# Norm vectors, dump tiles and memory tiles move into shared buffers, and the raw weight ring grows from three buffers to five

## The chip, the cores and the metric

The kernel runs on one core of a Trainium2 chip. The engines that matter here are TensorE (PE for its matmuls, PEld for its weight loads), VectorE (DVE), ScalarE (ACT), GpSimd (POOL), and SyncE (SP), whose queue issues nearly all DMA transfers. The metric is the device time in microseconds; for each kernel the median of several runs is compared. One further execution is profiled, and the profile and trace are of that one.

## The reference

A decoder trunk of four layers works on one sequence of 256 positions, 1024 wide, in float32. Each layer is a half-step SwiGLU feed-forward network (FFN), a token mixer that also attends to a memory of 256 rows, and a second half-step FFN, each between two RMS norms ("sandwich"). The mixer's kind changes with the layer (a gated spatial mix, dilated window attention, attention with forget gates, and the first again).

```python
def rms_norm(x, g):
    xf = x.astype(jnp.float32)
    y = xf * lax.rsqrt(jnp.mean(xf * xf, axis=-1, keepdims=True) + RMS_EPS)
    return (y * g.astype(jnp.float32)).astype(x.dtype)

def swiglu_ffn(x, w_gate_up, w_down):
    gate, up = jnp.split(x @ w_gate_up, 2, axis=-1)
    return (jax.nn.silu(gate) * up) @ w_down

def reference(...):
    for i in range(DEPTH):
        g = norm_g[i]
        x = x + 0.5 * rms_norm(swiglu_ffn(rms_norm(x, g[0]), ffn_w_gate_up[i, 0], ffn_w_down[i, 0]), g[1])
        h = rms_norm(x, g[2])
        mem_n = rms_norm(mem, mem_norm_g[i])
...
        x = x + rms_norm(y, g[3])
        x = x + 0.5 * rms_norm(swiglu_ffn(rms_norm(x, g[4]), ffn_w_gate_up[i, 1], ffn_w_down[i, 1]), g[5])
    return x
```

The FFN is 2816 wide. Every weight is read once; weights are most of the 360 MB that the kernel reads.

## The kernel before

**Weight units.** Weights arrive in units of 128 partitions by up to 1024 float32 (512 KB). A matmul in float32 precision is made of three faster ones: each weight is split into `hi` (ACT, line 309) and `lo` = weight - `hi` (DVE, line 310), and each activation likewise, and `hi*hi`, `hi*lo` and `lo*hi` are summed (`mm3`, lines 332 to 336; the FFN's down product at 684; the seven-product sets at 615). So each unit costs one DMA, one ACT and one DVE instruction, and 12 matmuls of 512 columns in most places.

**Two rings.** A unit is first loaded into a `raw` buffer (`RAW` = 3, `load_next`, line 242, issued by SP at line 240), then split into one of ten pairs `hi`, `lo` (`RING` = 10, `split_next`, line 288). Splitting a unit frees its raw buffer and issues the next load. `slot` (line 320) is called after each unit's matmuls: it releases ring places, issues one load of a quad if any is due, runs one job of the background list `bg`, and lets `pump` split up to two units, at most nine ahead of what PE has released.

**An FFN** (`ffn`, line 529) runs over six column sets of the gate and up weights, s = 0 to 5. Sets 0, 1, 3 take four gate and four up units each. Sets 2 and 4 (`SEVEN`) use a scheme of seven products instead of eight (`seven`, line 626): eight weight tiles ("quads", four tiles of two halves, loaded whole) are added and subtracted in place by DVE (line 277), and seven combinations are multiplied with prepared sums of activations (`sums`, line 593: S1 to S4, each split into a pair of tiles `sh`, `sl`). The quads live in the tiles tagged `rows`, `mgh`, `mgl` (of the main pool) and `q22` (of the FFN's own pool). In `seven` snapshots of partial sums go to four tiles tagged `snap`; `c11` (line 635), `c22`, `c21` and `c12` (lines 653 to 659) combine them on DVE. Set 5 has four mixed units (`half("e", ...)`, its product at line 719). Down products (22 units "D") are filled in between: 4 in set 1, 2 in set 3, 4 in each of the seven sets, and the last 8 at the end, which are held in the ring and passed over twice, first for the rows t = 0 and then for t = 1. Between the two passes `boundary` runs the norm for t = 0 and during the first units of what follows for t = 1.

**The norm** (`ln_stages`, line 356) has four steps: ACT squares the product into a `junk` dump, of which only the row sum is used (373), while DVE multiplies it by the vector `gpost` into `rows` (374); DVE adds it to x (378); ACT squares x into a dump (381); DVE scales by `gpre` into `rows` (385). POOL computes the reciprocal roots (348, 349). Then PE transposes `rows` (399). After mixers and after second FFNs the transposed result is also kept in four tiles `xf` of tag `snap`, for `sums`.

**Norm vectors.** `gain` (line 351) allots a tile `gpost` or `gpre` (one buffer each, in the main pool, 4 KB a partition) and issues a 512 KB load that repeats a vector over the partitions. In an FFN the job `gains` (line 667) is put on `bg` right after `sums`, in the first FFN after set 2; in a mixer both are loaded after the memory keys and values.

**Memory.** In the first FFN, after set 2, `setup2` (line 453) loads constants and the memory's rows (into the `gpost` buffer) and computes their norms. In each first FFN, after set 4, `mem_gained` (line 752) loads the transposed memory in eight pieces of 128 KB (`memraw`, two buffers) and splits them into `mgh`, `mgl`.

**What sets the order.** The program's order is a priority. The tile library lays out each engine's queue ahead of time from a model of durations and of buffers becoming free, so an instruction can stand earlier in its queue than in the text, but each queue runs in its order on the chip: an instruction that waits holds up all behind it. That includes SP's queue of loads.

Of the kernel before, what the change touches and what calls it, by code (L numbers as in the profile page):

```python
# [10 lines left out]
F32 = mybir.dt.float32  # L11
F32R = mybir.dt.float32r
I32 = mybir.dt.int32
BF16 = mybir.dt.bfloat16
AF = mybir.ActivationFunctionType
# [3 lines left out]
P = 128  # L19
SEQ = 256  # L20
D = 1024
# [11 lines left out]
RING = 10  # L33
RAW = 3
HELD = 8
# [168 lines left out]
class Trunk:  # L204
# [145 lines left out]

    def gain(self, l, n, tag):
        t = self.main.tile([P, D], F32, tag=tag, name=tag)
        self.nc.sync.dma_start(out=t, in_=self.io["norm_g"][l, n].partition_broadcast(P))
        return t

    def ln_stages(self, st, t, ps, post_scale, post_eps, gpost, gpre):
        nc = self.nc
        if "rows" not in st:
            st["rows"] = None
        junk = lambda: self.main.tile([P, D], BF16, tag="junk", name="junk")  # L360
        ss = self.small.tile([P, 1], F32, tag="ss", name="ss", bufs=8)
        r = self.small.tile([P, 1], F32, tag="r", name="r", bufs=8)
        ss2 = self.small.tile([P, 1], F32, tag="ss2", name="ss2", bufs=8)
        r2 = self.small.tile([P, 1], F32, tag="r2", name="r2")
        x = self.x[t]

        def rows():
            if st["rows"] is None:
                st["rows"] = self.main.tile([P, 2, D], F32, tag="rows", name="rows")
            return st["rows"][:, t, :]  # L370

        def s1():
            nc.scalar.activation(out=junk(), in_=ps, func=AF.Square, scale=post_scale, accum_out=ss)  # L373
            nc.vector.tensor_tensor(out=rows(), in0=ps, in1=gpost, op=ALU.mult)  # L374
            self.rsqrt(r, ss, post_eps)

        def s2():
            nc.vector.scalar_tensor_tensor(out=x, in0=rows(), scalar=r, in1=x, op0=ALU.mult, op1=ALU.add)  # L378

        def s3():  # L380
            nc.scalar.activation(out=junk(), in_=x, func=AF.Square, scale=1 / 32, accum_out=ss2)
            self.rsqrt(r2, ss2, self.eps1)

        def s4():
            nc.vector.scalar_tensor_tensor(out=rows(), in0=x, scalar=r2, in1=gpre, op0=ALU.mult, op1=ALU.mult)

        out = []
        if ps is not None:
            out += [s1, s2]
        if gpre is not None:  # L390
            out += [s3, s4]
        return out
# [36 lines left out]
    def setup(self):  # L429
# [3 lines left out]
        nc.sync.dma_start(out=self.x[0], in_=io["x"][:P, :])  # L433
        self.gpre = self.gain(0, 0, "gpre")
        nc.sync.dma_start(out=self.ident, in_=io["ident"])
# [17 lines left out]
    def setup2(self):  # L453
        nc, io, c = self.nc, self.io, self.const
        self.tri1 = c.tile([P, SEQ], F32, name="tri1")
        self.R = c.tile([P, SEQ], F32, name="R")

        def loads():
            nc.sync.dma_start(out=self.tri1, in_=io["tri1"])
            nc.sync.dma_start(out=self.mg, in_=io["mem_g"])  # L460

        def squares(t):
            m = self.main.tile([P, D], F32, tag="gpost", name="memrow")
            nc.sync.dma_start(out=m, in_=io["mem"][t * P:(t + 1) * P, :])
            ss = self.small.tile([P, 1], F32, tag="ss", name="ss", bufs=8)
            nc.scalar.activation(out=self.main.tile([P, D], BF16, tag="junk", name="junk"), in_=m, func=AF.Square,
                                 scale=1 / 32, accum_out=ss)
            self.rsqrt(self.r_mem[:, t:t + 1], ss, self.eps1)

        def inverse():  # L470
            ps = self.rot()
            for t in range(2):
                d = self.main.tile([P, SEQ], F32, tag="memraw", name="memf", bufs=2)
                nc.vector.tensor_scalar(out=d[:, :P], in0=self.ident, scalar1=self.r_mem[:, t:t + 1], scalar2=None,
# [54 lines left out]
    def ffn(self, l, f, post_next, pre_next, last=False):  # L529
        nc, tc = self.nc, self.tc  # L530
        with tc.tile_pool(name=f"ffn{l}{f}", bufs=1, reuse_waits="tile") as fp:
# [61 lines left out]
            def sums():  # L593
# [3 lines left out]
                for dst, a, b, op in ((x22, x21, x22, ALU.subtract), (x21, x11, x21, ALU.subtract),  # L597
                                      (x11, x22, x11, ALU.subtract), (x12, x12, x11, ALU.add)):
                    tt(out=dst, in0=a, in1=b, op=op)
                    y = tuple(fp.tile([P, 4, P], F32R, tag=n, name=n, bufs=4) for n in ("sh", "sl"))  # L600
                    self.split(*(v.rearrange("p a b -> p (a b)") for v in y), dst)
# [65 lines left out]
            def gains():  # L667
                gn["post"] = self.gain(l, post_next[0], "gpost")
                if pre_next:
                    gn["pre"] = self.gain(*pre_next, "gpre")  # L670

            if (l, f) != (0, 0):
                self.bg.append(gains)
            ys = [self.acc() for _ in range(2)]
# [26 lines left out]
            for s in range(1, SETS):  # L701
# [3 lines left out]
                if s in SEVEN:  # L705
                    seven(s)
                    if s == min(SEVEN) and (l, f) == (0, 0):
                        self.bg.extend(self.setup2() + [gains])
                    if s == min(SEVEN) and (l, f) == (0, 1):
# [37 lines left out]
    def mem_chunk(self, k):  # L747
        m = self.main.tile([P, SEQ], F32, tag="memraw", name="memraw", bufs=2)
        self.nc.sync.dma_start(out=m, in_=self.io["mem_t"][k * P:(k + 1) * P, :])
        return m  # L750
# [211 lines left out]
    def gains(self, l):  # L962
        return self.gain(l, 3, "gpost"), self.gain(l, 4, "gpre")

# [364 lines left out]
```

## Time and profile before

| | |
|---|---|
| median of 3 runs | 1900.68 us |
| lowest, highest run | 1900.43, 1908.29 us |
| the profiled execution's own time | 1902.04 us |
| span of its instructions | 1900.2 us |
| PE, DVE, ACT busy | 98%, 80%, 57% of the span |
| granted TensorE clock | 0.999 |
| DMA | 362.65 MB, mean 191 GB/s |
| raw loads, quad loads | 515, 128 |

The page gives busy shares, groups of instructions by line and a chain of work; other views of the same trace list waits, windows and the timeline. In a list of waits each row reads "engine, what it was about to write, line <- what ended the wait: total us, times, longest us". In a table of windows the columns are the window, the busy time of PE, PEld, DVE, ACT and POOL (with counts), the granted clock, the DMA engines' busy share and GB/s. A matmul's duration is modelled: consecutive matmuls overlap in the records.

### The profile page before, as it was taken

What the parts mean: (1) busy time and instruction counts of PE and PEld (TensorE: products, weight loads), DVE (VectorE), ACT (ScalarE), POOL (GpSimd) and SP (SyncE); (2) the same over time, 40 slices, a digit from 0 to 9 for tenths busy, and PEclk for the clock granted to TensorE, in tenths of its full rate; (3) what the DMA queues carried; (4) which work ended last, traced back from release to release, by engine and by line L of the source; (5) the groups of instructions that cost most, each with busy time, mean ns of one, the idle gap of its engine ahead of it and who ended that gap; (6) DMA issues with size and microseconds to landing.
All of it is one profiled execution on the core that took longest, in us unless ns stands there. A gap on an engine that the chain in (4) does not pass through costs nothing.

```text
span 1900.2 us, 25015 instructions
## 1 busy us (share of the span) xinstructions
PE 1858.8 (98%) x9406; PEld 1550.4 (82%) x9406; DVE 1514.9 (80%) x1828; ACT 1085.9 (57%) x1469; POOL 59.8 (3%) x115
## 2 busy tenths in 40 slices
PE   7999999999999999999999999999999999999998
PEld 5888888787878897888888889888888878988886
DVE  6987888896879768889697966878877886878894
ACT  5655656564656545655565656555556555656562
POOL 0000100000000000000000000000000000100000
PEclk9999999999999999999999999999999999999999
DMA  8646747545663663754566357275476535747632
GB/s 295 235 167 200 233 156 266 205 140 176 233 222 115 199 203 111 266 198 145 180 231 233 112 185 238 102 246 184 151 229 227 189 127 183 243 156 244 220 105 86
DMA packets 103865, 362.65 MB, mean 191 GB/s; under 512 B 12084, under 2 KB 16576, under 8 KB 103616
## 3 DMA queue, kind: packets, MB, share of 16 engines
q1 hardware_dynamic: 103568, 359.47, 56.5%
q8 instruction: 74, 1.21, 0.3%
q0 software_dynamic: 176, 1.59, 0.2%
q14 instruction: 47, 0.39, 0.1%
HBM read 359.95 MB, written 1.06 MB: 190 GB/s over the span
## 4 chain that ended last, share of the span: by engine, by line
PE 60%; DVE 17%; DMA 12%; ACT 5%; issue 4%; POOL 1%; ACTq 0%; SPq 0%; DVEq 0%
PE acc L684 15%; DMA raw<-in_w 12%; PE rot L615 9%; PE rot L334 9%; PE rot L336 9%; PE rot L335 9%; DVE lo L310 9%; ACT hi L309 4%; DVE quad L277 3%; PE acc L944 3%; PE rot L557 1%; PE rot L399 1%; PE rot L848 1%; DVE x L378 1%; PE rot L880 1%
## 5 line engine op out<-in xcount | busy, mean ns | idle before, releaser
L310 DVE TENSOR_TENSOR lo<-raw,hi 128x1024 fp32r<-128x1024 f32 (+1 forms) x515 | 624.4, 1219 | 216.9 <-ACT hi L309 207.5
L309 ACT ACTIVATE hi<-raw 128x1024 fp32r<-128x1024 f32 (+1 forms) x515 | 542.1, 1055 | 397.0 <-DMA raw<-in_w 259.0
L334 PE MATMUL rot<-hi,xth 128*128 128x512 f32 (+3 forms) x1072 | 414.9, 387 | 2.5 <-ACT hi L309 1.6
L336 PE MATMUL rot<-hi,xtl 128*128 128x512 f32 (+3 forms) x1072 | 411.6, 384 | 1.2 <-DVE xtl L310 1.1
L335 PE MATMUL rot<-lo,xth 128*128 128x512 f32 (+3 forms) x1072 | 411.6, 384 | 0.0
L309 ACT ACTIVATE hi<-quad 128x1024 fp32r<-128x1024 f32 x224 | 232.7, 1056 | 156.5 <-DVE quad L277 83.4
L310 DVE TENSOR_TENSOR lo<-quad,hi 128x1024 fp32r<-128x1024 f32 x224 | 269.4, 1220 | 7.2 <-ACT hi L309 6.2
L334 PEld LDWEIGHTS rot<-hi,xth 128*128 128x128 f32 x1072 | 202.1, 189 | 41.4 <-ACT hi L309 2.1
L336 PEld LDWEIGHTS rot<-hi,xtl 128*128 128x128 f32 x1072 | 201.9, 188 | 41.3 <-DVE xtl L310 2.3
L335 PEld LDWEIGHTS rot<-lo,xth 128*128 128x128 f32 x1072 | 202.1, 189 | 38.2
L684 PE MATMUL acc<-lo,hh 128*128 128x512 f32 x640 | 198.9, 390 | 0.0
L684 PE MATMUL acc<-hi,hh 128*128 128x512 f32 x640 | 198.0, 390 | 0.0
L684 PE MATMUL acc<-hi,hl 128*128 128x512 f32 x640 | 197.2, 389 | 0.0
L277 DVE TENSOR_TENSOR quad<-quad 128x1024 f32<-128x1024 f32 x128 | 154.2, 1220 | 0.9
L684 PEld LDWEIGHTS acc<-hi,hl 128*128 128x128 f32 x640 | 120.1, 188 | 25.0 <-DVE hl L310 0.2
L684 PEld LDWEIGHTS acc<-lo,hh 128*128 128x128 f32 x640 | 120.2, 188 | 24.8
L684 PEld LDWEIGHTS acc<-hi,hh 128*128 128x128 f32 x640 | 119.5, 188 | 24.3
L615 PE MATMUL rot<-hi,sh 128*128 128x512 f32 x256 | 103.0, 402 | 6.8 <-DVE snap L635 6.8
L615 PE MATMUL rot<-lo,sh 128*128 128x512 f32 x256 | 100.0, 391 | 0.0
L615 PE MATMUL rot<-hi,sl 128*128 128x512 f32 x256 | 97.4, 390 | 0.0
L374 DVE TENSOR_TENSOR rows<-acc,gpost 128x1024 f32<-128x1024 f32 x24 | 29.3, 1222 | 74.9 <-ACT junk L373 74.8
L615 PE MATMUL rot<-hi,xtl 128*128 128x512 f32 x192 | 74.8, 389 | 0.0
(212 smaller groups left out, 2439.8 us busy)
## 6 DMA issues: line engine op xcount, KB each, us to landing
raw<-in_w SPq DMA_DIRECT2D x504, 512.0 KB, 4.3
quad<-in_w SPq DMA_DIRECT2D x128, 512.0 KB, 5.8
gpre<-in_norm_g SPq DMA_DIRECT2D x12, 512.0 KB, 5.1
gpost<-in_norm_g SPq DMA_DIRECT2D x12, 512.0 KB, 5.4
memraw<-in_mem_t SPq DMA_DIRECT2D x32, 128.0 KB, 3.2
raw<-in_w SPq DMA_DIRECT2D x8, 384.0 KB, 3.5
sw<-in_sw SPq DMA_DIRECT2D x2, 768.0 KB, 8.1
cb<-cd POOLq DMA_DIRECT2D x1, 1536.0 KB, 9.9
```

Source lines behind the costliest of these rows:

```text
L277: add = lambda x, y: self.nc.vector.tensor_tensor(out=x, in0=x, in1=y, op=ALU.add)
L309: self.nc.scalar.activation(out=hi, in_=src, func=AF.Copy)
L310: self.nc.vector.tensor_tensor(out=lo, in0=src, in1=hi.bitcast(F32), op=ALU.subtract)
L334: mm(out, a[0], b[0], start=start, stop=False)
L335: mm(out, a[0], b[1], start=False, stop=False)
L336: mm(out, a[1], b[0], start=False, stop=stop)
L374: nc.vector.tensor_tensor(out=rows(), in0=ps, in1=gpost, op=ALU.mult)
L378: nc.vector.scalar_tensor_tensor(out=x, in0=rows(), scalar=r, in1=x, op0=ALU.mult, op1=ALU.add)
L399: nc.tensor.transpose(ps[:, (k - k0) * P:(k - k0 + 1) * P], rows[:, k * P:(k + 1) * P], self.ident)
L615: nc.tensor.matmul(ps, a[i], w[j][:, kk, :], start=fresh and h == kk == i == j == 0, stop=h == kk == i == 1, skip_group_check=True)
L684: mm(ys[t][:, n * 512:(n + 1) * 512], x, y[:, 0, n * 512:(n + 1) * 512], start=(j == 0 and x is a[0] and y is w[0]), stop=(j == NF - 1 and ...
L944: self.nc.tensor.matmul(o["y"][t][:, h * 512:(h + 1) * 512], x, y[:, 0, h * 512:(h + 1) * 512], start=(j == 0 and x is a[0] and y is w[0]) ...
```

## The change

- `RAW` goes from 3 to 5.
- In an FFN, `gpost` and `gpre` are allotted from tag `S` of the FFN's pool: four tiles that first hold the sums S1 to S4 (`sh` and `sl` become the two halves of one tile). The job `gains` is put on `bg` after set 4 in every FFN.
- In a mixer, the two vectors get tiles of the mixer's own pool. The very first `gpre` lies in half of an `mgh` tile.
- The dumps of the squares (`dump`), `memf` and `memraw` use the four `snap` tiles.
- The memory's rows become the two halves of a `rows` tile, and `setup2` is put on `bg` after set 4, behind `gains`, instead of after set 2.

```diff
-RAW = 3
+RAW = 5
...
-    def gain(self, l, n, tag):
-        t = self.main.tile([P, D], F32, tag=tag, name=tag)
+    def dump(self):
+        return self.main.tile([P, D], BF16, tag="snap", name="junk", bufs=4)
+
+    def gain(self, l, n, t):
         self.nc.sync.dma_start(out=t, in_=self.io["norm_g"][l, n].partition_broadcast(P))
         return t
...
-            nc.scalar.activation(out=junk(), in_=ps, func=AF.Square, scale=post_scale, accum_out=ss)
+            nc.scalar.activation(out=self.dump(), in_=ps, func=AF.Square, scale=post_scale, accum_out=ss)
...
-            nc.scalar.activation(out=junk(), in_=x, func=AF.Square, scale=1 / 32, accum_out=ss2)
+            nc.scalar.activation(out=self.dump(), in_=x, func=AF.Square, scale=1 / 32, accum_out=ss2)
...
-        self.gpre = self.gain(0, 0, "gpre")
+        self.gpre = self.gain(0, 0, self.main.tile([P, 2, D], F32, tag="mgh", name="gpre")[:, 0, :])
...
         def squares(t):
-            m = self.main.tile([P, D], F32, tag="gpost", name="memrow")
+            if t == 0:
+                both.append(self.main.tile([P, 2, D], F32, tag="rows", name="memrow"))
+            m = both[0][:, t, :]
...
-                d = self.main.tile([P, SEQ], F32, tag="memraw", name="memf", bufs=2)
+                d = self.main.tile([P, SEQ], F32, tag="snap", name="memf", bufs=4)
...
-                    y = tuple(fp.tile([P, 4, P], F32R, tag=n, name=n, bufs=4) for n in ("sh", "sl"))
+                    y = fp.tile([P, 2, 4, P], F32R, tag="S", name="sums", bufs=4)
+                    y = (y[:, 0], y[:, 1])
...
             def gains():
-                gn["post"] = self.gain(l, post_next[0], "gpost")
+                tile = lambda n: fp.tile([P, D], F32, tag="S", name=n, bufs=4)
+                gn["post"] = self.gain(l, post_next[0], tile("gpost"))
                 if pre_next:
-                    gn["pre"] = self.gain(*pre_next, "gpre")
-
-            if (l, f) != (0, 0):
-                self.bg.append(gains)
+                    gn["pre"] = self.gain(*pre_next, tile("gpre"))
+
...
-                    if s == min(SEVEN) and (l, f) == (0, 0):
-                        self.bg.extend(self.setup2() + [gains])
+                    if s == max(SEVEN):
+                        self.bg.append(gains)
+                    if s == max(SEVEN) and (l, f) == (0, 0):
+                        self.bg.extend(self.setup2())
...
-        m = self.main.tile([P, SEQ], F32, tag="memraw", name="memraw", bufs=2)
+        m = self.main.tile([P, SEQ], F32, tag="snap", name="memraw", bufs=4)
...
-        return self.gain(l, 3, "gpost"), self.gain(l, 4, "gpre")
+        return tuple(self.gain(l, n, self.mp.tile([P, D], F32, name=f"g{n}")) for n in (3, 4))
```

## What the change will do to the time: the prediction

> **What bounds the kernel now.** I read the page's first two lines, then the waits of the matmul engine, then the windows around the worst of those waits, and last the queue that issues the loads.
>
> ```profile
> span 1900.2 us, 25015 instructions
> PE 1858.8 (98%) x9406; PEld 1550.4 (82%) x9406; DVE 1514.9 (80%) x1828; ACT 1085.9 (57%) x1469; POOL 59.8 (3%) x115
> ```
>
> Columns are busy time, share of the span, count. The matmul engine is the bound: it is idle for 1900.2 - 1858.8 = 41.4 us, and no change to buffers can give more than that. The waits of PE (total us, times, longest) say who owns the idle time:
>
> ```profile
> PE rot L399 <- DVE rows L385: 15.5, 11, 8.4
> PE rot L615 <- DVE snap L635: 6.8, 7, 1.8
> PE rot L557 <- DVE T L659: 4.8, 6, 1.5
> PE rot L557 <- DVE T L719: 2.1, 5, 0.7
> PE rot L334 <- ACT hi L309: 1.6, 1, 1.6
> ```
>
> The first row is the norm chain: 8.4 us are the start of the kernel, and 15.5 - 8.4 = 7.1 us are ten waits at the ends of stages. Weight buffers do not touch it. The other four rows are the stock that this change can draw on: 6.8 + 4.8 + 2.1 + 1.6 = 15.3 us. They are a little too small, because a matmul's end is modelled:
>
> ```profile
> 381.94 0.39 PE L335 MATMUL rot<-lo,xth 128*128 128x512 f32 x1
> 382.16 0.39 PE L336 MATMUL rot<-hi,xtl 128*128 128x512 f32 x1
> 383.29 1.09 PE L557 MATMUL rot<-ident,T 128*128 128x128 f32 x8 [0.74 <-DVE T L659]
> ```
>
> Matmuls start about 0.225 us apart but are drawn 0.39 long, so each wait hides 0.39 - 0.225 = about 0.165 us. With 7, 6, 5 and 1 waits the stock is 8.0, 5.8, 2.9 and 1.8 us, 18.5 us in all. A weight unit of 12 such matmuls lasts about 12 x 0.225 = 2.7 us.
>
> Why is DVE late at these places? One case, the PE wait at 383, on DVE and on ACT:
>
> ```profile
> 380.31 1.06 ACT L309 ACTIVATE hi<-raw 128x1024 fp32r<-128x1024 f32 x1 [1.63 <-DMA raw<-in_w]
> 381.40 1.22 DVE L310 TENSOR_TENSOR lo<-raw,hi 128x1024 fp32r<-128x1024 f32 x1 [0.86 <-ACT hi L309]
> 382.55 0.68 DVE L659 TENSOR_TENSOR T<-T,snap 128x512 f32<-128x512 f32 x1
> ```
>
> The product T that PE needs stands in DVE's queue behind a split, the split waits for ACT's hi, and hi waits 1.63 us for a raw weight. The late party is a DMA. Over the whole kernel that is ACT's largest wait:
>
> ```profile
> ACT hi L309 <- DMA raw<-in_w: 259.0, 226, 3.7
> raw<-in_w SPq DMA_DIRECT2D x504, 512.0 KB, 4.3
> quad<-in_w SPq DMA_DIRECT2D x128, 512.0 KB, 5.8
> ```
>
> The windows of one FFN (layer 0, second; PE, PEld, DVE, ACT, POOL busy, clock, DMA share, GB/s) show the shape that matters:
>
> ```profile
> 306.00:330.00 24.00, 24.00 (x112) 19.96 (x111) 18.08 (x22) 15.11 (x18) 0.00 (x0) 1.00 0.83 265
> 330.00:348.00 18.00, 18.00 (x81) 14.92 (x80) 18.00 (x18) 8.41 (x10) 0.00 (x0) 1.00 0.00 0
> 348.00:366.00 18.00, 16.24 (x76) 13.19 (x75) 15.56 (x16) 11.78 (x14) 0.00 (x0) 1.00 0.93 330
> 366.00:384.00 18.00, 17.26 (x81) 14.08 (x80) 12.44 (x13) 9.58 (x12) 0.00 (x0) 1.00 0.72 256
> 425.00:452.00 27.00, 27.00 (x125) 22.45 (x124) 17.63 (x18) 14.28 (x18) 0.00 (x0) 1.00 0.72 232
> 456.00:468.00 12.00, 12.00 (x54) 9.92 (x54) 5.09 (x5) 5.34 (x7) 1.72 (x3) 1.00 0.15 46
> ```
>
> First DVE has 24.00 - 18.08 = 5.9 us without work while weights arrive; then it is busy without a break while the DMA engines stand still for 18 us (all three raw buffers are full and the products read quad tiles instead); then the loads come in a burst, and PE loses 1.76 and 0.74 us. Work that DVE could not do in the first window is what it is late with in the third.
>
> **The change, part by part.**
>
> *RAW 3 to 5.* No instruction is added: each split still issues one load, and setup issues two more ahead. A raw buffer's turn is landing 4.3 us, hi and lo, and an issue:
>
> ```profile
> L310 DVE TENSOR_TENSOR lo<-raw,hi 128x1024 fp32r<-128x1024 f32 (+1 forms) x515 | 624.4, 1219 | 216.9 <-ACT hi L309 207.5
> L309 ACT ACTIVATE hi<-raw 128x1024 fp32r<-128x1024 f32 (+1 forms) x515 | 542.1, 1055 | 397.0 <-DMA raw<-in_w 259.0
> 320.64 26.82 SPq L240 DMA_DIRECT2D raw<-in_w  x4
> 349.39 0.33 SPq L240 DMA_DIRECT2D raw<-in_w  x1
> ```
>
> That is 4.3 + 1.06 + 1.22 + 0.33 = 6.9 us. Three buffers give one unit per 2.3 us against PE's 2.7: a lead that the quad stage has eaten comes back by only 0.4 us per unit. With quads in the queue, 5.8 us to landing, it is 8.4 / 3 = 2.8 us, and no lead is won. Five give 1.4 and 1.7 us, about what the burst's 330 GB/s allow (0.524 MB / 330 GB/s = 1.6 us). Also, two more units (1.05 MB, 3.2 us of the burst) load while the queue now stands still (four issues in 26.82 us).
>
> The landings spread widely (raws and quads together):
>
> ```profile
> DMA to landing us min/median/max: 2.9/4.4/8.9
> ```
>
> At the shortest, 2.9 us, three buffers already give a unit per (2.9 + 1.06 + 1.22 + 0.33) / 3 = 1.8 us, win 0.9 us of lead per unit, and need no help; that is the second rival. [...]
>
> *Norm vectors.* In an FFN, gpost and gpre move from buffers of their own to two of the four tiles of the sums (tag S), and the two loads move from the FFN's start to after its second seven-product set.
>
> ```profile
> gpre<-in_norm_g SPq DMA_DIRECT2D x12, 512.0 KB, 5.1
> gpost<-in_norm_g SPq DMA_DIRECT2D x12, 512.0 KB, 5.4
> SPq L353 <- DVE rows L385: 11.8, 6, 2.0
> ```
>
> Removed from the FFN's start, where loads are short: 1.05 MB, 3.2 us of DMA time by 330 GB/s, and a wait of the issuing queue of up to 2.0 us behind which raw loads stand. Added at the end: the same 3.2 us, in a stretch like 425 to 452, where 0.28 x 27 = 7.6 us of DMA time are free; then comes 456 to 468 at 0.15. Needed is gpost about 19 us after its issue (three more units of 2.7 us and eight half units of 1.35), against 5.4 us to land. So 0 us; if that cover is gone, at most 3.2 us per FFN. The loads wait for the readers of two S tiles, products of the same set, long done when PE reaches the units issued behind them. In the mixers the two vectors get tiles of their own; nothing there waits longer.
>
> *Dumps, memraw and memf in the snap tag.* Same instructions, same durations; only who waits for whom. Dumps are written and followed by ACT in its own order. The memory chunks get up to four buffers for two, shared with snapshots that are read by then:
>
> ```profile
> SPq L749 <- DVE mgl L761: 24.2, 14, 4.6
> ```
>
> Between a gain of a few us on that queue (it is not PE's time) and a stall of one load; I take 0.
>
> *Memory rows in the rows tag, setup2 after the second seven set, in the first FFN only.* Loads of 1.05 MB rows, 0.14 MB constants and the 1.05 MB of norm vectors leave the first row's stretch for the second's:
>
> ```profile
> 60.00:80.00 20.00, 20.00 (x94) 16.67 (x93) 19.42 (x19) 12.02 (x16) 1.66 (x4) 1.00 0.37 134
> 147.00:182.00 35.00, 35.00 (x161) 29.02 (x159) 27.40 (x35) 20.97 (x28) 0.00 (x0) 1.00 0.73 234
> ```
>
> 2.2 MB are 6.8 us at 330 GB/s; free are 0.27 x 35 = 9.5 us. The cost lies between 0 and 6.8 us; nearer 0, since they fit, but ACT's two squares stand in order before splits and PE's two small products behind those: I take 1.2 us.
>
> *First gpre in mgh, sh and sl as one tile.* A quad pair can go into mgh once the last read of the first gpre is over:
>
> ```profile
> 11.58 1.28 DVE L385 SCALAR_TENSOR_TENSOR rows<-x,r,gpre 128x1024 f32<-128x1024 f32 x1 [1.08 <-POOL r L349]
> 10.90 0.91 SPq L240 DMA_DIRECT2D quad<-in_w  x2
> 0.00:20.00 20.00, 9.68 (x29) 7.23 (x30) 8.40 (x8) 9.63 (x13) 1.85 (x11) 1.00 0.85 285
> L309 ACT ACTIVATE hi<-quad x224: 1041/1061/1067, 56.5 to 1840.4; 128x1024 fp32r<-128x1024 f32 x112
> ```
>
> That is at 12.9 us, 2 us after the first quads' issue at worst, and the last row above has the first split of a quad at 56.5 us; the sums cost the same two instructions each. 0 us.
>
> **The sum.** Of the L635 stock (8.0 us, all in the quad stages, where DVE's own load also counts) I take three quarters, 6.0: the data come about 6 us earlier (3.2 from the prefetch, 3.2 from the norm vectors), DVE has 5.9 us free to use it, and the longest wait is 1.8. Of L659 (5.8 us, latency) three quarters, 4.4. Of L719 (2.9 us, where the norm vectors now arrive) a third, 1.0. Of the start's 1.8 us, 1.3, since five units are under way at once but the DMA engines are already 0.85 busy in the first 20 us. Gain 12.7, cost 1.2, net 11.5 us. The profiled execution took 1902.04 us (span 1900.2 and 1.8 around it): 1890.5. The median of the runs, 1900.68, lies 1.4 below that execution; so I forecast **1889.2 us**, with 1883 to 1894 as the forecast's own range.
>
> **The rivals.**
>
> 1. *DVE is the bound of the quad stage, not the loads* (0.26). For: DVE is busy 18.00 of 18 us from 330 to 348 with no load under way, and extra raws cannot add DVE time; and hi also waits because the ring of ten split units is full, the first row below being the largest such wait. Against: 5.9 us of DVE idle time just before. Then L635 stays and L659 gives half: 2.9 + 1.0 + 1.3 less 1.2 = 4.0, so 1896.7 us.
> 2. *The depth brings nothing* (0.12): three buffers turn fast enough, as at the shortest landing above, or the issuing queue's order, laid out ahead, keeps quads ahead of the two extra raws, so that the change does not do what it says. Then only the norm vectors' move counts, about a quarter of L635, 2.0, less 1.2: 1899.9 us. [...]
> 3. *Slower: late loads starve the end of each FFN* (0.08). From 425 to 452 the DMA share is 0.72 and raws are already late; 1.05 MB in one issuing queue put every raw behind them back by 3.2 us. It decides once PE's lead in split units falls under 3.2 us, about 1.2 units. Seven FFNs at 3.2 us, and 6.8 in the first, are 29 us less the gain of 12.7: 1917 us. Against: five raws make up lead faster than three.
> 4. *Everything in the stock goes* (0.04): 18.5 us, 1882.2 us.
>
> ```profile
> ACT hi L309 <- PE acc L684: 56.6, 53, 2.3
> ```
>
> **How the numbers follow.** The forecast has 0.50. About 0.5% (9.5 us: under 1891.2) is what a measurement of this kernel can tell from no change. Of the forecast's range some four fifths lie below that, 0.40, and with rival 4 and an edge of rival 1 faster has 0.50; the rest of the forecast and rivals 1 and 2 make 0.42 within; slower is rival 3, 0.08. The range leaves out rival 3, rival 4's lower part and the far edge of rival 2: 1882.5 to 1900.
>
> **What would show it.** Right: PE's waits for L635 fall from 6.8 to about 2 us and for L659 from 4.8 to about 1; ACT's 259 us for raw loads fall by over a third; the stretch of no DMA traffic in the quad stage begins later and DVE idles less before it; norm-vector loads are issued late in each FFN and nobody waits for them. Rival 1: ACT's wait for raws falls, L635 stays. Rival 2: ACT's wait hardly changes. Rival 3: new PE waits for hi or lo in the last set and the down products. A wait on gpost, or longer norm chains (L385 over 15.5), would prove the moved vectors wrong.

## The result and the profile after

The changed kernel takes 1880.31 us (median of 4 runs, 1880.14 to 1881.38); the kernel before, on the same chip, 1902.38 (4 runs, 1900.43 to 1908.29). The ratio is 0.988, 95% interval 0.9856 to 0.9904: about 22 us. The forecast was 1889.2, 11.5 us under the 1900.68 us known then; the result lies 2 us under the range's lower end. The profiled execution took 1880.4 us, and its span is 21.6 us shorter than before's 1900.2.

The first two lines of the changed kernel's page (busy time, share, count), and the share of each engine in the chain that ended last:

```profile
span 1878.6 us, 25126 instructions
PE 1854.1 (99%) x9406; PEld 1550.5 (83%) x9406; DVE 1516.5 (81%) x1828; ACT 1091.8 (58%) x1471; POOL 65.5 (3%) x115
...
PE 90%; DVE 4%; DMA 2%; issue 1%; ACT 1%; POOL 1%; SPq 0%; ACTq 0%; DVEq 0%
```

The same chain line of the page before:

```profile
PE 60%; DVE 17%; DMA 12%; ACT 5%; issue 4%; POOL 1%; ACTq 0%; SPq 0%; DVEq 0%
```

PE does the same 9406 matmuls and is idle for 1878.6 - 1854.1 = 24.5 us, before 41.4. Of the chain, 12% were DMA and 17% DVE; 2% and 4% are left. The chain now runs through PE alone for nine tenths of the span.

All waits of PE after the change (total us, times, longest; the lines moved by one to seven: L399 is now L400, L635 is L641, L659 is L665, L719 is L726):

```profile
PE rot L400 <- DVE rows L386: 15.1, 11, 8.1
PE rot L562 <- DVE T L726: 1.2, 2, 0.8
PE rot L334 <- ACT hi L309: 0.4, 1, 0.4
PE rot L335 <- DVE lo L310: 0.3, 1, 0.3
```

The norm chain stands as it was (15.5 before). The waits for the snapshots (6.8 us) and for the product T of L659 (4.8 us) are not smaller, they are gone. Four rows of before that the prediction didn't list are gone too:

```profile
PE rot L336 <- DVE xtl L310: 1.1, 1, 1.1
PE rot L334 <- ACT xth L309: 0.8, 1, 0.8
PE rot L334 <- DVE mgl L310: 0.6, 1, 0.6
PE rot L848 <- DVE p L902: 0.5, 1, 0.5
```

Listed waits fell from 33.8 us (34 times) to 17.0 (15 times). With 0.165 us for each wait, the prediction's estimate of what one hides, that is 16.8 + 19 x 0.165 = 19.9 of the 21.6 us. The last 1.7 us belong to no row.

ACT's largest waits after the change show what limits the split ring now:

```profile
ACT hi L309 <- PE rot L336: 188.6, 133, 3.4
ACT hi L309 <- PE acc L689: 110.0, 85, 2.0
```

Both mean that all ten split units are full and ACT waits until PE has used one up. Before, the first row was the wait for raw weights, 259.0 us; that wait is now a small one, as the row below shows. Loads are ahead of PE, not behind it.

```profile
ACT hi L309 <- DMA raw<-in_w: 27.0, 40, 2.4
```

The same FFN in windows (columns as in the prediction: length, then PE, PEld, DVE, ACT, POOL busy, clock, DMA share, GB/s). It begins some 6 us earlier, so these windows answer to before's from 306 on:

```profile
300.00:324.00 24.00, 24.00 (x112) 19.96 (x111) 22.52 (x26) 14.20 (x17) 0.00 (x0) 1.00 0.68 239
324.00:342.00 18.00, 18.00 (x81) 14.92 (x80) 17.73 (x30) 8.49 (x9) 0.00 (x0) 1.00 0.23 72
342.00:360.00 18.00, 17.92 (x84) 14.60 (x83) 15.54 (x27) 16.56 (x21) 0.00 (x0) 1.00 0.79 288
360.00:378.00 18.00, 18.00 (x85) 15.01 (x84) 15.19 (x16) 11.46 (x13) 0.00 (x0) 1.00 0.82 279
378.00:396.00 18.00, 18.00 (x81) 14.88 (x81) 17.96 (x20) 8.52 (x9) 0.00 (x0) 1.00 0.01 5
```

DVE works 22.5 of 24 us in the first window, where it had 18.1 before: 4.4 us of work have moved ahead. Then the two burst windows lose 0.08 us of PE instead of 1.76 + 0.74. DVE is still busy for nearly all of the two quad stages (17.73 and 17.96 of 18 us, one for each seven-product set), and PE loses nothing there.

### The profile page after: what moved, and what is told of

Its sections match the earlier page's. It is cut to its first block, busy times and chain, and to the rows that moved or that the text cites. A ratio compares the mean times of both kernels' runs of the same rounds, so it can differ in the third digit from the quotient of the medians.

```text
span 1878.6 us, 25126 instructions
## 1 busy us (share of the span) xinstructions
PE 1854.1 (99%) x9406; PEld 1550.5 (83%) x9406; DVE 1516.5 (81%) x1828; ACT 1091.8 (58%) x1471; POOL 65.5 (3%) x115
## 4 chain that ended last, share of the span: by engine, by line
PE 90%; DVE 4%; DMA 2%; issue 1%; ACT 1%; POOL 1%; SPq 0%; ACTq 0%; DVEq 0%
PE acc L689 22%; PE rot L621 15%; PE rot L334 14%; PE rot L335 14%; PE rot L336 14%; PE acc L951 3%; PE rot L562 2%; DMA memraw<-in_mem_t 1%; DVE lo L310 1%; PE rot L400 1%; PE rot L855 1%; PE acc L873 1%; ACT hi L309 1%; PE rot L887 1%; DMA raw<-in_w 1%
## 5 line engine op out<-in xcount | busy, mean ns | idle before, releaser
L309 ACT ACTIVATE hi<-raw 128x1024 fp32r<-128x1024 f32 (+1 forms) x515 | 536.1, 1052 | 263.2 <-PE acc L689 87.8
L334 PE MATMUL rot<-hi,xth 128*128 128x512 f32 (+3 forms) x1072 | 415.1, 387 | 0.4 <-ACT hi L309 0.4
L334 PEld LDWEIGHTS rot<-hi,xth 128*128 128x128 f32 x1072 | 202.0, 188 | 39.1 <-ACT hi L309 0.8
L621 PE MATMUL rot<-hi,sums 128*128 128x512 f32 x512 | 168.9, 396 | 0.1
L621 PEld LDWEIGHTS rot<-hi,sums 128*128 128x128 f32 x512 | 96.1, 188 | 24.3 <-DVE snap L641 4.8
L621 PE MATMUL rot<-lo,sums 128*128 128x512 f32 x256 | 99.9, 390 | 0.0
L348 POOL TENSOR_TENSOR r<-ss,thin 128x1 f32<-128x1 f32 x48 | 23.4, 488 | 1582.9 <-ACT junk L374 1490.3
```

The lines of the kernel that those rows point to most:

```text
L309: self.nc.scalar.activation(out=hi, in_=src, func=AF.Copy)
L334: mm(out, a[0], b[0], start=start, stop=False)
L348: g.tensor_tensor(out=out, in0=ss, in1=eps_tile, op=ALU.add)
L621: nc.tensor.matmul(ps, a[i], w[j][:, kk, :], start=fresh and h == kk == i == j == 0, stop=h == kk == i == 1, skip_group_check=True)
```

## The experiments

Two theories could explain the gain. **Refill**: five buffers turn, so by the estimated turn of 6.9 us a raw unit comes every 1.4 us where it came every 2.3. **Prefetch and move**: two more units are loaded while the issuing queue stands still, and the norm vectors leave the FFN's start. A third question is what the moves into shared tiles cost by themselves; the prediction had them at 1.2 us. Ratios are to the kernel before, run on the same chip, with 95% intervals; not all groups ran on one chip, so ratios are compared, not times, where two groups meet.

### The shared tiles with three and four buffers

The changed kernel with the old number, and with one more:

```diff
-RAW = 5
+RAW = 3        # e1_moves_only;  RAW = 4 in e2_raw4
```

> The changed kernel with three raw buffers again: all tiles share buffers and the norm vectors and the first memory work come late, but no depth is added. Theory D (the two more raw buffers do most of it, by loading in the stretch without DMA traffic and by refilling the ring faster): the moves take 1.05 MB out of each FFN's start and no more, so 1895 to 1899 us, PE still waits about 4 to 6 us for L641 (the line that was L635) and 3 to 5 us for the product before the transposes, and ACT waits over 180 us for raw loads. Theory V (the norm vectors leaving the crowded start do most of it): 1881 to 1888 us, those two PE waits together under 3 us, and ACT's wait for raw loads well under 150 us.

> The changed kernel with four raw buffers. Theory D: half the depth brings more than half the gain, since the turn of a buffer, 6.9 us, over four is 1.7 us, already near the 1.6 us that the DMA engines allow: 1882 to 1888 us, ACT's wait for raw loads 60 to 130 us. Theory V: the same as with three and with five buffers within 3 us, 1880 to 1885. If depth counts in proportion: half way between the kernel with three and the one with five.

| buffers, all moves made | us | ratio |
|---|---|---|
| 3 | 1916.94 | 1.0091 (1.006 to 1.0121) |
| 4 | 1893.25 | 0.9955 (0.9941 to 0.9969) |
| 5 (the change) | 1880.31 | 0.988 (0.9856 to 0.9904) |

The moves alone make the kernel slower by 0.9%, about 17 us. The first extra buffer brings 0.0136 x 1900 = 26 us, the second 0.0075 x 1900 = 14 us. So the change is a loss of some 17 us and a gain of some 40, not a gain of 12.7 and a loss of 1.2.

PE's waits with three buffers (all of the list):

```profile
PE rot L400 <- DVE rows L386: 16.7, 14, 8.2
PE rot L562 <- DVE T L726: 7.4, 9, 1.4
PE acc L873 <- ACT qm L839: 6.9, 2, 3.8
PE rot L621 <- DVE snap L641: 4.0, 3, 2.1
PE rot L562 <- DVE T L665: 2.8, 4, 1.3
PE rot L335 <- DVE lo L310: 2.3, 2, 1.9
PE rot L334 <- DVE mgl L310: 1.0, 1, 1.0
PE rot L481 <- DVE hl L310: 0.8, 1, 0.8
```

They sum to 41.9 us, 8.1 more than before. The span is 1915.9, 15.7 more. The rest shows in windows right behind the longest waits, in the clock column:

```profile
82.00:86.00 4.00, 4.00 (x12) 3.10 (x11) 4.00 (x6) 1.13 (x2) 0.00 (x0) 0.57 0.75 249
86.00:90.00 4.00, 4.00 (x19) 3.31 (x18) 2.23 (x3) 2.42 (x4) 0.00 (x0) 1.00 0.98 379
...
243.00:250.00 7.00, 5.39 (x25) 4.56 (x25) 6.15 (x10) 6.24 (x13) 0.55 (x1) 0.52 0.72 225
...
1677.00:1684.00 7.00, 6.31 (x30) 5.49 (x31) 6.67 (x11) 5.51 (x13) 0.15 (x1) 0.55 0.81 222
```

PE is busy for 4 us in the first row and starts 12 matmuls; one window later it starts 19. The granted clock is 0.57, 0.52 and 0.55 in the three windows. I count what is missing to 1.00 only while PE works; by this estimate the loss is 0.43 x 4.00 + 0.48 x 5.39 + 0.45 x 6.31 = 7.1 us. Waits and clock make 8.1 + 7.1 = 15.2 of the 15.7 us. Two stalls, in the first and the last mixer (PE waits for ACT's qm), are paid a second time by this count.

With four buffers ACT's wait for raw weights is 91.4 us, between 248.5 with three and 27.0 with five.

### The norm vectors at the FFN's start again

With four and with three buffers, vectors loaded early into tiles of their own:

```diff
-                tile = lambda n: fp.tile([P, D], F32, tag="S", name=n, bufs=4)
+                tile = lambda n: fp.tile([P, D], F32, name=n)
...
+            if (l, f) != (0, 0):
+                self.bg.append(gains)
```

> Four raw buffers, and the norm vectors of every FFN but the first load at its start again, into tiles of their own, so that nothing waits for an old vector. The difference to the run with four buffers and late vectors is the move alone. Theory D: 1 to 4 us slower than that run (3.2 us of DMA time at each of seven starts, most of it covered by the added depth). Theory V: 8 us slower or more, 1890 to 1898 us.

> Three raw buffers, shared tiles, but the norm vectors of all FFNs but the first loaded at the start again. Against the run with three buffers and late vectors (1916.9) it tells whether late vectors starve an FFN's end when the ring is shallow. If they do (PE's wait before the last transposes, 7.4 us there against 2.1 before): 1908 to 1912 us, that wait back near 2 us. If they do not: 1914 to 1919 us. At 1900 us the whole loss of that run would be theirs.

With four: 1891.91 us, 0.9963 (0.9949 to 0.9976), against 0.9955 with the vectors late. With three: 1916.82 us, 1.0058 (1.0042 to 1.0074), against 1.0091 (1.006 to 1.0121). Where the two loads stand makes no difference that shows with four. Taking them out of the FFN's start, where the prediction had counted 3.2 us of earlier data, brought nothing that shows. With three the intervals meet; the late place is not better there either. Both kernels change the vectors' tiles together with the time; a kernel further on (e17) changes the time alone.

### An extra load at the FFN's start

If traffic at the FFN's start matters with five buffers, more of it must cost. The changed kernel loads 0.64 MB more, which nothing reads, at the start of seven FFNs:

```diff
+            def extra():
+                t = fp.tile([P, 1250], F32, name="extra")
+                g = self.io["norm_g"][l].rearrange("n d -> (n d)")[:1250]
+                nc.sync.dma_start(out=t, in_=g.partition_broadcast(P))
+
+            if (l, f) != (0, 0):
+                self.bg.append(extra)
```

> The changed kernel, five raw buffers, with one extra load of 0.64 MB into a tile that nobody reads at the start of every FFN but the first (the vectors' real loads stay late). It puts 61% of the traffic back at the place that the change has emptied. Theory D: five buffers cover it, 1880 to 1883 us, PE waits for L641 under 2 us in all. Theory V: 61% of the loss comes back, 1888 to 1894 us.

1895.38 us, 0.9972 (0.9962 to 0.9983): 15 us lost by the medians, 17 by the ratios. That is more than either theory gave, and it is not in waits. PE's four rows of waits sum to 17.2 us, after's to 17.0. The group row of the down products (busy, mean ns of one) has it:

```profile
L696 PE MATMUL acc<-hi,hh 128*128 128x512 f32 x640 | 202.0, 397 | 0.0
```

```profile
L689 PE MATMUL acc<-hi,hh 128*128 128x512 f32 x640 | 197.9, 390 | 0.0
```

The first is this run, the second the change without the extra load: the same matmul, 397 ns for 390. The tile is 1250 x 4 = 5000 bytes in each partition, so every tile placed behind it starts elsewhere. Two more kernels part the load from the place: one loads into 1216 columns (4864 bytes, a multiple of 128), the other only makes the 5000-byte tile and writes one column of it, with no load.

> The last run of the first group with the extra tile 1216 numbers wide instead of 1250 (4864 bytes a partition, a multiple of 128, instead of 5000). In that run PE lost no more to waits than in the changed kernel, but its 512-column down products came 231 to 234 ns apart instead of 227. Theory A (the tiles behind the extra one were misplaced by 8 bytes and PE reads them more slowly; the traffic itself is covered by five buffers): 1880 to 1884 us and 227 ns again. Theory T (the 0.64 MB at the FFN's start cost the 15 us): 1892 to 1897 us.

> The changed kernel with a tile of 1250 numbers (5000 bytes a partition) in every FFN's pool but the first, of which POOL writes one column; nothing is loaded. Theory A (placement): 1890 to 1897 us, down products 231 to 234 ns apart, no new waits. Theory T (traffic): 1880 to 1882 us.

The load in an aligned tile: 1881.43 us, 0.9897 (0.986 to 0.9934), its matmuls as in the change:

```profile
L696 PE MATMUL acc<-hi,hh 128*128 128x512 f32 x640 | 197.9, 390 | 0.0
```

(Its profiled execution, 1886.18 us, had one wait of 3.3 us for a snapshot; the other three lie between 1879.23 and 1881.51.) The 5000-byte tile alone: 1892.32 us, 0.9957 (0.9942 to 0.9972):

```profile
L692 PE MATMUL acc<-hi,hh 128*128 128x512 f32 x640 | 202.0, 397 | 0.0
```

So five buffers cover 0.64 MB more at the FFN's start at no cost that shows in the median, and 12 of the 15 us (15 of 17 by the ratios) are the tile's place. It also speaks against the part of the forecast that came from moving the vectors.

### Prefetch or refill

First with the order in which loads are written down: three ahead outside the seven-product sets and five within (e7), or the opposite (e8):

```diff
+        self.depth = [5 if any(v[0] <= n <= v[-1] for v in at.values()) else 3 for n in range(len(self.plan))]
...
+    def top_up(self):
+        while len(self.raws) < self.depth[self.split_n] and self.loaded < len(self.raw_order):
+            self.load_next()
...
-            self.load_next()
+        self.top_up()
```

> Five raw buffers, but more than three are loaded ahead only between the first and the last split of a seven-product set, that is in the stretch where the queue stood still; elsewhere no load is issued while three are ahead. Theory P (the two units loaded in the idle stretch make the gain): at most 1890 us, ACT's wait for raw loads under 120 us. Theory F (the faster refill elsewhere makes it): 1903 to 1917 us, near the run with three buffers (1916.9), ACT's wait over 180 us. If both count alike: about 1898.

> The opposite: five loads ahead everywhere except from six units before a seven-product set to its last split, where three are the limit; so nothing more than before is loaded in the idle stretch. Theory F: at most 1888 us. Theory P: 1900 to 1917 us. If both count alike: about 1898.

1879.06 us, 0.9889 (0.9858 to 0.9919), and 1880.66 us, 0.9897 (0.9866 to 0.9927): both equal the change, and so does ACT's wait for raw weights: 26.2 and 21.5 us, against 27.0. This did not separate the theories. By the code the buffers still turn by fives; that the issuing queue runs ahead of the text's order until a buffer is missing is inferred, from the loads counted in e10's trace below (101 issued, 96 split). What it shows is that the planned order of loads mattered little here.

Then with the buffers themselves: each load takes the buffer that came free last, so that outside the chosen stretches only three really turn:

```diff
+        self.free = list(range(RAW))
...
-        t = self.wp.tile([P, 1024], F32, tag="raw", name="raw", bufs=RAW)
+        i = self.free.pop()
+        t = self.wp.tile([P, 1024], F32, tag=f"raw{i}", name="raw")
...
+            self.free.append(i)
+        self.top_up()
```

> The two runs before limited the loads in the order of the text, but the queue could still run ahead through five buffers. Here a load reuses the buffer freed last, so that outside the seven-product stretches only three buffers really turn; in the stretch two more are filled and held. Theory P (the idle stretch makes the gain): at most 1886 us. Theory F (faster refill makes it): 1900 to 1917 us. Theory M (depth is needed in the mixers as well, where the run with three buffers lost 11 us): 1888 to 1896 us, with the loss in the mixers and on ACT's query copy.

> The opposite with the same means: five buffers turn, but from six units before a seven-product set to its last split only three, so that nothing more than with three is loaded in the idle stretch. Theory F or M: 1880 to 1887 us. Theory P: 1895 to 1910 us, with PE's waits for L641 and for the product before the transposes back at 5 us or more each in the FFNs and none in the mixers.

| five buffers turn | us | ratio |
|---|---|---|
| only within the seven-product sets (e9) | 1914.41 | 1.0049 (1.0029 to 1.007) |
| only outside them and the six units ahead (e10) | 1882.13 | 0.9876 (0.9859 to 0.9894) |

e10 was meant to be the refill without the prefetch, but its trace has the prefetch as well. Loads of raw weights issued, and split by ACT, up to 332 us, inside the quiet stretch of layer 0's second FFN (count, then shortest, median and longest in ns, then first and last start):

```profile
L246 SPq DMA_DIRECT2D raw<-in_w x101: 327/328/797, 2.1 to 314.6; - x101
L321 ACT ACTIVATE hi<-raw x96: 1041/1060/1072, 8.1 to 311.8; 128x1024 fp32r<-128x1024 f32 x96
```

So 101 - 96 = 5 loads are held there. The change and e9 have the same 101 and 96, and three buffers (e1) have 99 and 96. It is the same in the other quiet stretches of e9 and e10. So the queue runs ahead of the text's order there, and the two buffers that e10 doesn't turn there are filled ahead all the same.

So e9 and e10 hold equally much in that stretch, and they differ in what turns outside it. e9 is the prefetch without the refill, and is near three buffers everywhere (1916.94 us, 1.0091): the prefetch alone is worth 2.5 us by the medians and 8 by the ratios, whose intervals meet. e10 has both and the whole gain. The refill is therefore needed for most of the gain; whether it would bring all of it without the two loads held ahead is not shown. ACT's wait for raw weights, first in e9, then in e10:

```profile
ACT hi L321 <- DMA raw<-in_w: 221.2, 180, 4.5
```

```profile
ACT hi L321 <- DMA raw<-in_w: 93.8, 67, 4.0
```

In e10 ACT still waits 93.8 us for loads, but PE's waits stay at four rows, T L738 (L726 of the change) the only one that grew, to 2.4 us. These waits of ACT cost PE next to nothing, presumably because PE had split units in store.

### What the moves cost, one at a time

Each on the kernel before with its three buffers: dumps in the snapshot tag (e13), memory chunks and memf there (e14), late norm vectors of the FFNs in the tiles of the sums (e15), both memory rows in the rows tag with setup2 after the second seven-product set (e16). The edits are those parts of the diff, nothing else; e13's is

```diff
-        junk = lambda: self.main.tile([P, D], BF16, tag="junk", name="junk")
+        junk = lambda: self.main.tile([P, D], BF16, tag="snap", name="junk", bufs=4)
```

> The kernel before with one part of the change: the dumps of the squares rotate through the four snap tiles. The change with three buffers was 17 us slower than before, and early vectors or the mixers' vectors did not explain it. If this part carries it: 1910 us or more, with a PE wait on ACT's query copy in both mixers of the first kind. If the loss is the sum of small shifts in the order that the library lays out: within 5 us of before, 1896 to 1906.

> The kernel before with the memory chunks and the two memf tiles in the four snap tiles. If this part carries the loss (more chunk loads can be issued ahead of raw loads): 1908 us or more, with PE's wait before the last transposes of the first FFNs up from 2.1 us. Otherwise 1896 to 1906.

> The kernel before with sums in one tile a pair and the FFNs' norm vectors in them, loaded late; the mixers' vectors and all else as before. By my prediction's term it gains 2 us (a quarter of L635): 1897 to 1900. If late vectors starve a shallow ring at the end of an FFN: 1905 to 1912 us and PE's wait before the last transposes at 5 us or more.

> The kernel before with the memory's rows in the rows tile and the first memory work after the second seven-product set of the first FFN. By my prediction's term it costs 1.2 us, within 0 to 6.8: 1901 to 1907, all of it before 200 us. If it carries the loss of the mixers: 1910 us or more.

| move | us | ratio |
|---|---|---|
| dumps | 1898.59 | 0.9998 (0.9978 to 1.0018) |
| memory chunks | 1907.86 | 1.0041 (1.0021 to 1.006) |
| norm vectors | 1912.25 | 1.0065 (1.0042 to 1.0088) |
| memory rows | 1904.33 | 1.002 (1.0007 to 1.0034) |

The sum is 1.24%; all moves together cost 0.9%, so the parts don't simply add. In e14 the row that grew most is PE's wait for the product T of L719 (before 2.1 us), while those for L635 and L659 fell to 4.8 and 2.3 us:

```profile
PE rot L557 <- DVE T L719: 6.7, 8, 1.4
```

In e15 it is the first mixer. PE's wait, and a window there:

```profile
PE acc L872 <- ACT qm L838: 7.6, 2, 4.7
```

```profile
240.00:247.00 7.00, 2.33 (x11) 1.35 (x10) 5.64 (x9) 4.05 (x5) 0.55 (x1) 0.70 0.78 236
```

and the same window of the kernel before:

```profile
240.00:247.00 7.00, 7.00 (x58) 6.58 (x58) 5.66 (x11) 5.90 (x13) 0.15 (x1) 1.00 0.77 234
```

PE works 2.3 of 7 us there. On ACT's timeline of e15 the splits ahead of qm wait for raw weights:

```profile
240.56 1.06 ACT L309 ACTIVATE hi<-raw 128x1024 fp32r<-128x1024 f32 x1 [1.06 <-DMA raw<-in_w]
243.23 1.06 ACT L309 ACTIVATE hi<-raw 128x1024 fp32r<-128x1024 f32 x1 [1.62 <-DMA raw<-in_w]
```

Is that because the vectors load late, or because of the tile they are in? e17 loads them late, into the buffers of their own that the kernel before has:

```diff
-            if (l, f) != (0, 0):
-                self.bg.append(gains)
...
-                        self.bg.extend(self.setup2() + [gains])
+                        self.bg.extend(self.setup2())
+                    if s == max(SEVEN):
+                        self.bg.append(gains)
```

> The kernel before with only the time of the norm vectors' loads changed: late in every FFN, but into their old tiles in the main pool. The run with late vectors in the sums' tiles was 0.65% slower than before, 7 us of its profiled loss in the first mixer, on ACT's query copy. If the place decides (tiles of the FFN's pool, read until its end, under the mixer's tiles): ratio within 0.998 to 1.002 and no such wait in the first mixer. If lateness decides (1.05 MB in front of the mixer's loads while the ring is shallow): ratio 1.004 to 1.008 with that wait.

1898.97 us, 0.9992 (0.9973 to 1.0011), and the wait for qm is nearly away:

```profile
PE acc L866 <- ACT qm L832: 0.2, 1, 0.2
```

Late is free; what costs is the tiles: the place of the vectors, or that S1 to S4 each become one tile, which e15 changes too. In e15 the vectors lie in the FFN's own pool until the last norm of the FFN has read them, on space that the next mixer's tiles take over. That link is inferred from the code. Which tile waits, and how it makes raw weights late 30 us on, I have not shown. A last kernel tried the mixers' own two vectors as the cause, in the shared layout with three buffers:

```diff
-        return tuple(self.gain(l, n, self.mp.tile([P, D], F32, name=f"g{n}")) for n in (3, 4))
+        return tuple(self.gain(l, n, self.main.tile([P, D], F32, tag=f"g{n}", name=f"g{n}")) for n in (3, 4))
```

> Three raw buffers and the changed kernel's late vectors in the FFNs, but the mixers' two vectors in tiles of the main pool instead of the mixer's own, so that the mixer's tiles lie as before. If their place and time of loading cause the stalls on ACT's query copy (4.0 and 3.2 us, and the half clock after them): 1905 to 1909 us and no wait of that kind over 1 us. If not: 1914 to 1919 us with those stalls still there.

1915.78 us, 1.0062 (1.0036 to 1.0088), the wait for qm still 9.2 us: not they.

No kernel beat the change beyond the intervals. Six buffers, and the old layout with four or five, weren't tried; so what the moves still cost beside five buffers stays open.

## Why the prediction was wrong in size

**The bound and the stock: right, but cut short.** PE is the bound, and the gain came from the waits that the prediction named. But the stock of 18.5 us left out the four smaller rows (3.0 us, 3.7 with what waits hide), without a reason. After the change all four are gone.

**The step that failed: the sizes in the sum.** "Of the L635 stock I take three quarters ... Of L659 three quarters ... Of L719 a third." By the waits after, with 0.165 us added for each:

| term | taken | measured |
|---|---|---|
| L635, 8.0 us | 6.0 | 8.0 |
| L659, 5.8 us | 4.4 | 5.8 |
| L719, 2.9 us | 1.0 | 2.9 - 1.5 = 1.4 |
| start's hi, 1.8 us | 1.3 | 1.8 - 0.6 = 1.2 |
| small rows, 3.7 us, less the new 0.5 for lo | 0 | 3.2 |
| norm chain | 0 | 0.4 |
| memory rows | -1.2 | no row |
| sum of the rounded parts | 11.5 | 20.0 |

The sum is 8.5 us too small: 3.7 by the fractions, 3.2 by the small rows that it left out, 1.2 by a cost of the memory rows that no wait of PE shows, 0.4 by the norm chain. The 0.165 us that the measured column adds for each wait is the prediction's own estimate.

The fraction for L635 was put down to DVE's own load, that for L719 to the norm vectors arriving there; that for L659 was given without a reason. The trace of before spoke against the first: its DVE was idle for 5.9 us ahead of a longest wait of 1.8, and after the change it had used up 4.4 us of that. Here the lead won, 4.4 us, was larger than the longest wait, and the wait fell to zero, not to a quarter.

**Where the lead comes from: the source without a term.** The prediction gave the data's 6 us to the prefetch and to the vectors' move. e9 has the prefetch and gains 2.5 to 8 us on three buffers, of some 40; by e3 and e17 the time at which the vectors load is worth nothing that shows. The refill, a unit per 6.9 / 5 = 1.4 us instead of 2.3 against PE's 2.7, was in the text, but no term of the sum was made from it. Its working is in line with the runs: the lead won per unit is 0.4 us with three buffers, 1.0 with four, 1.3 with five, rising by 0.6 and 0.3, and the runs give 26 and 14 us for the two steps. That is two steps with one proportion, not a law.

**The costs of the moves: wrong at three buffers, not visible at five.** Dumps cost 0, as written. Memory chunks (0 taken) cost 0.4%, the vectors (0 taken) 0.65%, the memory rows (1.2 us taken) 0.2%, about 4 us, all beside three buffers. In e15 the splits ahead of PE's wait in the first mixer come late for want of raw weights, as the timeline shows; for the other two the way is not shown. With five buffers ACT's wait for raw weights is 27 us instead of 259; what the moves still cost there is not known.

**The rivals.** Rival 1 had its fact right (DVE busy 17.73 and 17.96 of 18 us) and its conclusion wrong: L635 went to zero. Rival 2 falls with e1 and e2: at the real landings (medians 4.3 and 5.8 us, not the shortest, 2.9) depth is what counted, and the vectors' move it rested on is worth nothing that shows. Rival 3 named late loads at the end of each FFN. Its sign is that of the moves alone, its cause is not: e17 has the loads late and loses nothing, and after the change no operation waits for a vector. The multiply by gpost shows it (what its engine waited for):

```profile
L375 DVE TENSOR_TENSOR rows<-acc,gpost x16: 1214/1224/1225, 184.8 to 1872.3; 128x1024 f32<-128x1024 f32 x16
...
  ACT junk L374: 61.7, 9
```

No DMA is among its releasers. Rival 4, everything in the stock goes, 1882.2 us, was the nearest, and had 4 in 100. That it came so near is in part luck: 1.4 us of its stock stayed for L719, and 3.2 us came from rows that it doesn't count.

**What would show it.** L635 and L659 fell past the forecast (about 2 and 1) to zero, and ACT's wait for raw weights by nine tenths where a third was asked. DVE idles less ahead of the quad stage, as said. The stretch without traffic was to begin later; it begins earlier. The last traffic of the kernel before (from 330 us on the prediction's window shows none), then the change's, where the same work comes some 6 us earlier:

```profile
326.00:330.00 4.00, 4.00 (x20) 3.30 (x19) 4.00 (x6) 4.00 (x6) 0.00 (x0) 1.00 0.54 186
```

```profile
318.00:322.00 4.00, 4.00 (x20) 3.30 (x19) 4.00 (x5) 1.11 (x3) 0.00 (x0) 1.00 0.39 140
322.00:336.00 14.00, 14.00 (x64) 11.58 (x63) 13.97 (x19) 5.72 (x6) 0.00 (x0) 1.00 0.00 1
```

So the two extra units are not loaded while the queue stands still: all five are there, and the traffic stops, some 3 us sooner.

## What to carry to other kernels

Judge the depth of a load ring by its turn (landing, both uses, issue) over the number of buffers, against the consumer's time per unit (here 6.9 us over five, 1.4, against 2.7); if that wins more lead than the longest wait, count nearly the whole stock of waits behind late loads, small rows too (here 20 us, where 11.5 were taken). When space for it comes from sharing tiles, price the sharing at the old depth as well: here it cost 17 us with three buffers. When an experiment is meant to hold loads back, count in its trace the loads that are out. And after adding a tile, look at the mean duration of matmuls that don't touch it (here 397 ns for 390).

## What the runs showed of the hardware

**A tile's place changed the matmul's speed.** With a 5000-byte tile ahead of the others, the down products with a 512-column operand went from 390 to 397 ns in the rows above, and the kernel took 12 us longer without the load and 15 us with it; with 4864 bytes they did not change. The gate and up products of L334 kept theirs, 393 to 394 ns: by the code their operands lie outside the FFN's pool, where the tile is, while the activations of the down products lie in it. So the activations' place is the likely cause. At what multiple, and by what mechanism, wasn't tried.

**Stalls of some 2 us were often followed by a stretch at half clock.** In such a stretch 512-column matmuls start 0.43 us apart, behind it 0.23, as in the four-buffer kernel's timeline:

```profile
82.48 0.63 PE L621 MATMUL rot<-lo,sums 128*128 128x512 f32 x1
82.91 1.06 PE L621 MATMUL rot<-hi,sums 128*128 128x512 f32 x2
...
84.74 0.39 PE L621 MATMUL rot<-lo,sums 128*128 128x512 f32 x1
84.97 0.62 PE L621 MATMUL rot<-hi,sums 128*128 128x512 f32 x2
```

By the clock column the three-buffer kernel runs at half speed from 82 us for 3.4 us (0.43 x 4.00 / 0.5), behind a wait of 2.1 us, and in the same way from 243 and 1677 us for 6.8 us each, beginning inside waits of 3.8 and 3.1 us. The four-buffer kernel has one stretch behind a wait of 1.9 us, below, and one of 3.4 us from 241 us, behind a wait of 2.1 us:

```profile
80.00:84.00 4.00, 4.00 (x11) 3.17 (x12) 3.27 (x5) 1.51 (x2) 0.00 (x0) 0.57 0.97 359
```

It has none behind a longer wait, of about 3 us, in the last mixer:

```profile
1650.00:1656.00 6.00, 3.03 (x26) 2.78 (x27) 5.93 (x11) 3.78 (x5) 0.68 (x1) 1.00 0.83 277
1656.00:1660.00 4.00, 4.00 (x35) 3.67 (x32) 3.38 (x6) 2.79 (x6) 0.57 (x1) 1.00 0.70 254
```

In e10 two shorter waits close together stood ahead of one:

```profile
1100.52 0.41 PE L574 MATMUL rot<-ident,T 128*128 128x128 f32 x2 [1.32 <-DVE T L738]
1101.58 0.41 PE L574 MATMUL rot<-ident,T 128*128 128x128 f32 x2 [0.65 <-DVE T L738]
1102.00:1106.00 4.00, 4.00 (x12) 3.10 (x12) 1.23 (x3) 0.38 (x1) 0.00 (x0) 0.57 0.26 69
```

By the windows such a stretch costs half of the time that PE works in it, an estimate of 1.7 us for those of 3.4 us and 2.6 and 2.8 us for the two of 6.8, on top of the stall; before's waits for snapshots, 1.8 us at most, had none: its clock is 1.00 until 1880 us. What sets the length of a stretch, and why the last mixer's wait had none, is not shown.
